# Mixture-of-experts weights: from two-part products on the whole TensorE to float32 products on four 32-column tiles

## The chip, the core and the metric

One core of a Trainium2 chip runs the whole program. The metric is the device time of one execution in microseconds (us). A profile of one execution shows every instruction of the engines: PE is TensorE's matmuls, PEld its weight loads, DVE is VectorE, ACT is ScalarE, POOL is GpSimd, and SP issues the transfers from HBM.

## What is computed

A decoder trunk of two layers over 256 tokens of width 1024. Each layer has a mixer (a gated spatial part and an attention), a channel part, two norms and a gate. The channel part of layer 0 is a dense SwiGLU; that of layer 1 is eight SwiGLU experts, of which every token uses two:

```python
def swiglu(x, w1, w3, w2):
    return (jax.nn.silu(x @ w1) * (x @ w3)) @ w2

def moe(x, w_r, w1, w3, w2):
    ...
    top_l, top_i = lax.top_k(logits, TOP_K)
    top_w = jax.nn.softmax(top_l, axis=-1)
    combine = jnp.sum(jax.nn.one_hot(top_i, N_EXPERTS, dtype=jnp.float32) * top_w[..., None], axis=1)
    ...
    for e in range(N_EXPERTS):
        out = out + combine[:, e:e + 1] * swiglu(xt, w1[e], w3[e], w2[e])
```

An expert's three matrices are 1024 x 3584, 1024 x 3584 and 3584 x 1024, in float32: 44 MB, and 352 MB for all eight. With the inputs of the reference the experts have 74, 61, 64, 40, 50, 69, 94 and 60 tokens.

## The kernel before

The tokens lie in two blocks of 128. A class `Stream` (line 96) holds the order in which all weights are used. A unit of up to 1 MiB is loaded into a buffer of a ring (`load`, line 186), and `take` (line 202) hands out its pieces, 128 rows by 1024 columns each. `_split` (line 127) cuts a piece into two parts of 12 significant bits, high and low: ScalarE copies it to the type fp32r (line 143), VectorE subtracts that copy from the piece (line 145). Both go to one of nine `cut` slots. A raw buffer is free once its last piece is cut, a slot once its piece has been multiplied.

A product of activations and weights is then three fp32r matmuls per 512 columns (`mm3`, line 426: activations' high part by weights' high part, high by low, low by high). In the trace they are the lines L428, L430 and L432; the weights' parts are `hl`.

The experts are computed in `moe` (line 974), one after the other. `gather_block` (line 939) multiplies the tokens by a 0/1 matrix, so that an expert's tokens stand in 128 slots, transposed (`g`, then `xg` in two parts). The hidden width of 3584 is done in 7 chunks of 512. `up` (line 1007) takes 8 pieces, each with 512 columns of w1 and the same of w3, into two PSUM banks (`m`), and makes `mh` = silu times product. `turn` transposes it (`mt`) and `turned` splits it (`mhT`). `down` (line 1030) takes 4 pieces of w2 into two more banks (`py`). `down` of a chunk stands behind `up` of the next, so that `mh` is made while `py` is computed. After an expert's last chunk, `spread` (line 1046) brings its rows back to the tokens (`sc`) and adds them to `acc`. One expert is thus 7 x (8 + 4) = 84 pieces, all eight 672, and a piece costs six matmuls of 512 columns.

PE, DVE and ACT run their instructions in the order of the program, which a scheduler has set; SP issues a unit's transfers when a buffer is free. A branch at the end, `overflow` (line 1102), handles tokens beyond an expert's slots; here no expert has more than 128.

Of the kernel before, what the change touches and what calls it, by code (L numbers as in the profile page):

```python
# [18 lines left out]
P = 128  # L19
# [39 lines left out]
RAW3 = 2  # L59
# [11 lines left out]
LEND = 3  # L71
LEND0 = 4
# [13 lines left out]
SPLITS = 4  # L86
AFT = 1
# [8 lines left out]
class Stream:  # L96
    """Weights in order of use: units of up to 1 MiB are loaded ahead, then cut, piece by piece, into two parts of 12
    significant bits each. Both token blocks take every piece, block 1 some pieces after block 0."""

    def __init__(self, tc, nc, raw, cut):  # L100
        self.tc = tc
        self.nc, self.rings, self.cut = nc, [raw], cut
        self.idle, self.busy, self.lend, self.lent = list(range(SPL)), {}, 0, []
        self.extra = []
        self.room, self.size = [RAW], [RAW]
        self.units, self.pieces, self.lags, self.stays = [], [], [], set()
        self.left = [None]
# [7 lines left out]
        self.highs, self.lows = [], []  # L115

    def add(self, srcs, cuts, gains=None, lag=1):
        """A unit without cuts is only loaded, and stays."""
# [8 lines left out]
    def _split(self, v):  # L127
        u, c0, c1, gain, last = self.pieces[v]
        t, n, nc = self.raws[u], c1 - c0, self.nc
        slot = self.busy[v] = self.idle.pop(0)  # L130
# [19 lines left out]
        if last:  # L150
            r = self.ring.pop(u)
            if isinstance(r, int):
                self.room[r] += 1
            elif r[0] == "cut":
                self.idle.append(r[1])
                self.lent.remove(r[1])
            del self.raws[u]
        self.tiles[v] = (hi, lo)

# [6 lines left out]
    def raw_tile(self, name, stays=False, dtype=F32):  # L166
        """a buffer of a ring that has room, or None."""
# [18 lines left out]
    def load(self, end=None):  # L186
        """Loads the next units, as far as there is room."""
# [10 lines left out]
    def give_back(self):  # L198
        for v in [v for v in self.busy if v < min(self.pos)]:
            self.idle.append(self.busy.pop(v))  # L200

    def take(self, b):
# [3 lines left out]
        while self.n_split < min(j + self.ahead, len(self.pieces) if self.limit is None else self.limit) and self.idle:  # L206
# [10 lines left out]
def side_by_side(st, gens):  # L217
    """Both blocks' programs, block 0 some pieces ahead."""
# [10 lines left out]
def trunk(ctx: ExitStack, tc: tile.TileContext, a, out):  # L229
# [56 lines left out]
    NC = D_FFE // CH  # L286
    steps = [(e, c) for e in range(NE) for c in range(NC)]
    for i in range(DEPTH):
# [15 lines left out]
        else:  # L304
            add_wide(a["ple_w_p"][i], [0], LAG_E)
            st.limit = len(st.pieces) if LIM else None
            def down(e, c):
                add_wide(a["moe_w2"][0, e][c * CH:(c + 1) * CH], range(0, CH // P, 2), 1)
            for s, (e, c) in enumerate(steps):
                add_pair(a["moe_w1"][0, e], a["moe_w3"][0, e], c * CH, CH, 1)  # L310
# [60 lines left out]
    def tables():  # L371
        """gains as columns, the mask, the rotary tables (tokens on partitions)."""
# [27 lines left out]
    def inv_root(name, v, n):  # L400
        """(v + eps) ** -0.5 of [P, n]."""
# [13 lines left out]
    def transposed(name, src, into, k0=0, nk=KT):  # L415
        """token-major [P, nk * P] -> two parts of its transpose."""
# [17 lines left out]
    def product(b, ps, xT, ks, between=iter(()), bias=None):  # L434
        """ps (two banks) = x_b @ w (+ bias, a row); the stream's next pieces are w's rows ks; other work's steps in between."""
# [19 lines left out]
    def half_product(b, ps, xT, between=iter(())):  # L455
        """ps (one bank) = x_b @ w, two rows of tiles in a piece."""
# [11 lines left out]
    def load_rows(key, *srcs):  # L468
        """vectors side by side, on every partition."""
# [34 lines left out]
    def embed_input(i, b, pT):  # L504
        """p[i] of the block, transposed, in two parts."""
# [6 lines left out]
    def embed(i, b, pp):  # L512
        """pp = p[i] @ ple_w_p[i]."""
# [6 lines left out]
    def mixer(i, b, xT):  # L520
        """x_b after the first residual and norm, and its transpose."""
# [53 lines left out]
        if b == 0:  # L575
            # the spatial gate's weights, masked and transposed
# [73 lines left out]
        m = gp.tile([P, 512], F32, name=f"{L}m{b}")  # L650

        def attend():
# [120 lines left out]
    def gated(b, ps, pp, xb):  # L773
        """xb += sigmoid(ps) * pp; the last layer's xb goes out."""
# [8 lines left out]
    def tail(i, b):  # L783
        """second norm and the per-layer embedding's gate."""
# [15 lines left out]
    def program(b):  # L800
        for i in range(DEPTH):
# [4 lines left out]
            else:  # L806
                if YR:
                    yield
                with tc.high_priority(offset=B_ROUTER) if b in BR else nullcontext():
# [4 lines left out]
                    placed = gather_block(tc, b, 0, x, early, rt["pg"], rt)  # L814
                if b == 1:
                    st.limit = None
                    st.after = [] if not LIM else [L_[i]["ends"][1]] * AFT + [placed.ins] * (SPLITS - AFT)
# [16 lines left out]
    moe(tc, a, st, x, acc, xtp, rt, early, ident, const, small, ps_mm, ps_tr, ps_s, mm3, split_from, steps)  # L834
# [8 lines left out]
    def finish(b):  # L843
        """the last norm and gate; acc stays."""
# [17 lines left out]
    def redo(w):  # L862
        """the last norm and gate once more, in whole float32 products."""
# [22 lines left out]
def router_constants(tc, a, rt, const):  # L886
# [6 lines left out]
    # places count from 1  # L893
# [20 lines left out]
def router(tc, b, rt, const, ps_tr):  # L914
    """Every token's two experts and its place among each one's tokens, block after block."""
# [15 lines left out]
    # a token's place among its expert's tokens, from 1 on; 0 where it isn't one  # L931
# [7 lines left out]
def gather_block(tc, b, e, x, pl, pg, rt):  # L939
    """Adds the block's tokens of expert e to the two banks pg, transposed, each in its slot."""  # L940
    nc = tc.nc
    # 1 where a token of the expert stands in a slot
    placed = nc.vector.tensor_scalar(pl[:, b, :], rt["iota"], rt["slot"][:, b, e:e + 1], None, op0=OP.is_equal)
    for k in range(KT):
        # a bank's first product clears it
        nc.tensor.matmul(pg[k // 4][:, k % 4 * P:(k % 4 + 1) * P], lhsT=x[b][:, k * P:(k + 1) * P], rhs=pl[:, b],
# [4 lines left out]
def router_weights(tc, rt, small, const, ps_tr):  # L951
    """The softmax of the two logits, and the largest number of tokens of an expert."""
# [4 lines left out]
    # e = exp(second - first); weights 1 / (1 + e) and e / (1 + e)  # L957
# [16 lines left out]
def moe(tc, a, st, x, acc, xtp, rt, early, ident, const, small, ps_mm, ps_tr, ps_s, mm3, split_from, steps):  # L974
    """acc = alpha * x + experts(x), each expert on its own tokens."""
    nc = tc.nc
    iota, slot = rt["iota"], rt["slot"]
    with tc.tile_pool(name="moe", bufs=1) as mp:

        def gather(e, s):  # L980
            """expert e's tokens, transposed, in the banks of the step s."""
            pl = mp.tile([P, NB, P], F32, tag="place", name=f"place{e}")
            pg = [ps_mm(s % 2, f"g{e}_{q}") for q in range(2)]
# [4 lines left out]
        def gathered(e, pg):  # L988
            """in two parts."""
            xg = [mp.tile([P, KT, P], F32R, tag=f"xg{j}", name=f"xg{j}_{e}") for j in range(2)]  # L990
            for q in range(2):
                split_from(xg[0][:, q * 4:q * 4 + 4].rearrange("p k s -> p (k s)"), xg[1][:, q * 4:q * 4 + 4].rearrange("p k s -> p (k s)"), pg[q])
# [199 lines left out]
```

## Time and profile before

| | |
|---|---|
| median of three timed executions | 1485.36 us (1485.06 to 1485.43) |
| span of the profiled execution, first to last instruction | 1483.9 us |
| PE busy over the span | 1461.2 us, 98% |
| PEld, DVE, ACT busy | 80%, 82%, 66% |
| bytes read from HBM | 428.66 MB, 290 GB/s over the span |

The page's busy time of PE is the union of its matmuls' spans, and these overlap: a matmul is listed with its whole way through the array, while the next one has already begun. How fast PE really works is therefore read from the distance of two starts, not from a duration. The times in a timeline count from the start of the span.

### The profile page before, as it was taken

To read this page: it belongs to the slowest core of one execution; us is meant where nothing else is said; L and a number is where in the kernel's file an instruction comes from. 1 tells how busy PE (TensorE), PEld (TensorE's weight loads), DVE (VectorE), ACT (ScalarE), POOL (GpSimd) and SP (SyncE) were. 2 spreads that over 40 slices of the span, in tenths; PEclk is the share of its full clock that TensorE was granted. 3 is DMA by queue.
4 is the path that set the end of the run, shared out by engine and by line. 5 is a ranking of instruction groups with operands and counts; after the bars stand their busy time and mean duration, and the time that the engine had idled before them with its cause. 6 is when DMAs were issued, how large, how long until landed. Compare 5 with 4: busy or idle time off the path is not lost. (4 is left out here: it accounts for less than half of the span.)

```text
span 1483.9 us, 18910 instructions
## 1 busy us (share of the span) xinstructions
PE 1461.2 (98%) x6858; PEld 1188.8 (80%) x6858; DVE 1214.4 (82%) x1410; ACT 986.6 (66%) x1200; POOL 26.3 (2%) x55
## 2 busy tenths in 40 slices
PE   8999999999999999999999999999999999999997
PEld 7878888788878888888888888788878878887875
DVE  7876545588689989989988888998898899889876
ACT  6754444446468777777777677777677677767662
POOL 1000000000000000000000000000000000000000
PEclk9999999999999999999999999999999999999998
DMA  9535546565599999999999999999999899989820
GB/s 323 192 109 200 175 141 226 188 211 186 202 356 329 361 335 339 373 337 344 357 367 328 330 351 334 326 371 365 331 337 371 320 336 367 370 323 340 317 115 30
DMA packets 187311, 431.00 MB, mean 290 GB/s; under 512 B 12199, under 2 KB 18893, under 8 KB 187214
## 3 DMA queue, kind: packets, MB, share of 16 engines
q1 hardware_dynamic: 187214, 429.76, 80.4%
q8 instruction: 55, 0.90, 0.2%
q14 instruction: 42, 0.34, 0.1%
HBM read 428.66 MB, written 1.05 MB: 290 GB/s over the span
## 5 line engine op out<-in xcount | busy, mean ns | idle before, releaser
L145 DVE TENSOR_TENSOR hl<-raw,hl 128x1024 fp32r<-128x1024 f32 (+2 forms) x783 | 920.8, 1215 | 134.8 <-ACT hl L143 132.2
L143 ACT ACTIVATE hl<-raw 128x1024 fp32r<-128x1024 f32 (+2 forms) x783 | 787.6, 1049 | 214.0 <-PE m L432 62.7
L430 PE MATMUL m<-hl,xg 128*128 128x512 f32 x896 | 285.2, 397 | 1.1 <-DVE hl L145 1.1
L428 PE MATMUL m<-hl,xg 128*128 128x512 f32 x896 | 284.2, 397 | 0.0
L432 PE MATMUL m<-hl,xg 128*128 128x512 f32 x896 | 283.3, 396 | 0.0
L430 PEld LDWEIGHTS m<-hl,xg 128*128 128x128 f32 x896 | 167.6, 188 | 44.8 <-DVE hl L145 5.7
L432 PEld LDWEIGHTS m<-hl,xg 128*128 128x128 f32 x896 | 168.6, 188 | 40.4
L428 PEld LDWEIGHTS m<-hl,xg 128*128 128x128 f32 x896 | 167.3, 188 | 38.9
L428 PE MATMUL py<-hl,mhT 128*128 128x512 f32 x448 | 143.5, 401 | 0.2 <-ACT mhT L409 0.2
L430 PE MATMUL py<-hl,mhT 128*128 128x512 f32 x448 | 143.3, 401 | 0.0
L432 PE MATMUL py<-hl,mhT 128*128 128x512 f32 x448 | 140.9, 395 | 0.0
L432 PEld LDWEIGHTS py<-hl,mhT 128*128 128x128 f32 x448 | 84.2, 188 | 20.1
L430 PEld LDWEIGHTS py<-hl,mhT 128*128 128x128 f32 x448 | 82.1, 188 | 19.0 <-DVE hl L145 1.5
L428 PEld LDWEIGHTS py<-hl,mhT 128*128 128x128 f32 x448 | 81.9, 189 | 18.0 <-ACT mhT L409 0.7
L1015 ACT ACTIVATE mh<-m 128x512 f32<-128x512 f32 x56 | 33.3, 595 | 71.9 <-PE m L432 70.8
L409 ACT ACTIVATE mhT<-mt 128x512 fp32r<-128x512 f32 x56 | 33.4, 597 | 57.2 <-PE py L430 48.4
L1016 DVE TENSOR_TENSOR mh<-mh,m 128x512 f32<-128x512 f32 x56 | 38.4, 686 | 31.7 <-ACT mh L1015 31.5
L428 PE MATMUL ff<-hl,L0x1T 128*128 128x512 f32 (+1 forms) x192 | 57.6, 377 | 0.1
L430 PE MATMUL ff<-hl,L0x1T 128*128 128x512 f32 (+1 forms) x192 | 57.2, 373 | 0.0
L432 PE MATMUL ff<-hl,L0x1T 128*128 128x512 f32 (+1 forms) x192 | 56.3, 373 | 0.0
L409 DVE TENSOR_TENSOR mhT<-mt,mhT 128x512 fp32r<-128x512 f32 x56 | 38.5, 688 | 4.1 <-ACT mhT L409 2.6
L428 PEld LDWEIGHTS ff<-hl,L0x1T 128*128 128x128 f32 x192 | 35.0, 188 | 6.8 <-ACT L0x1T L409 0.5
(478 smaller groups left out, 1435.5 us busy)
## 6 DMA issues: line engine op xcount, KB each, us to landing
raw<-in_moe_w SPq DMA_DIRECT2D x448, 512.0 KB, 5.7
raw<-in_moe_w SPq DMA_DIRECT2D x112, 1024.0 KB, 6.6
raw<-in_ffn_w SPq DMA_DIRECT2D x40, 512.0 KB, 4.5
raw<-in_ffn_w SPq DMA_DIRECT2D x11, 1024.0 KB, 4.8
raw<-in_w_in SPq DMA_DIRECT2D x8, 1024.0 KB, 5.2
raw<-in_w_o SPq DMA_DIRECT2D x8, 1024.0 KB, 5.3
raw<-in_ple_w_g SPq DMA_DIRECT2D x8, 1024.0 KB, 4.9
raw<-in_w_in SPq DMA_DIRECT2D x4, 832.0 KB, 5.4
```

Source lines behind the costliest of these rows:

```text
L143: nc.scalar.activation(hi[:, :n], t[:, c0:c1], AF.Copy)
L145: nc.vector.tensor_tensor(lo[:, :n], t[:, c0:c1], hi[:, :n].bitcast(F32), op=OP.subtract)
L409: return nc.scalar.activation(hi, src, AF.Copy).ins, nc.vector.tensor_tensor(lo, src, hi.bitcast(F32), op=OP.subtract).ins
L428: nc.tensor.matmul(o, lhsT=xh, rhs=w, start=start, stop=False)
L430: nc.tensor.matmul(o, lhsT=xh, rhs=w, start=False, stop=False)
L432: nc.tensor.matmul(o, lhsT=xl, rhs=w, start=False, stop=stop)
L1015: nc.scalar.activation(hh, ps[0], AF.Silu)
L1016: nc.vector.tensor_tensor(hh, hh, ps[1], op=OP.mult)
```

## The change

Only the experts change. The host puts the three matrices of each expert into one array `moe_w`, in units of 1 MiB in the order of use, each unit 128 rows (one for each partition) of 8 KB without gaps (`expert_units`). The stream no longer cuts these pieces: `_split` hands out the raw buffer itself, and it is held until the piece has been multiplied (`whole`, `held`, `let_go`). The `cut` slots, which then stand idle, serve as buffers for loads (LEND and LEND0 are 9).

The products become plain float32 matmuls. An expert has 96 slots in place of 128, and they are three groups of 32. The array's 128 columns are used as four tiles of 32 columns: three of them hold the three groups of tokens, and the fourth holds one of these groups again, for another quarter of the weights. Of a piece's 1024 columns, three quarters of 256 columns (`main`) are multiplied by the three groups each, and the last quarter (`side`) by one group at each of the three turns. So a piece is 3 x 4 = 12 float32 matmuls of 256 columns.

The hidden width is done in chunks of 1024, 1024, 1024 and 512 in place of seven of 512; `up` of 1024 uses four PSUM banks. The rows of an expert go back to the tokens (`spread`) one step later, in float32.

```diff
@@ class Stream
+        if v in self.whole:
+            self.tiles[v] = (t[:, c0:c1], None)
+            if last:
+                self.held[v] = self.ring.pop(u)
+                del self.raws[u]
+            return
...
+        for v in [v for v in self.held if v < min(self.pos)]:
+            self.let_go(self.held.pop(v))
@@ trunk
-RAW3 = 2
+RAW3 = 1
...
-LEND = 3
-LEND0 = 4
+LEND = 9
+LEND0 = 9
...
+            def whole(e, units, cuts):
+                n = len(st.pieces)
+                for u in units:
+                    st.add([(lambda t: t, a["moe_w"][0, e, u])], cuts, None, 1)
+                st.whole.update(range(n, len(st.pieces)))
@@ moe
+        def tiles4(main, side, lhsT, wa, wb, start, stop):
+            for j in range(3):
+                for g in range(NG):
+                    nc.tensor.matmul(main[j][g], lhsT=lhsT(g), rhs=wa[j], start=start and j != 1, stop=stop, skip_group_check=True)
+                nc.tensor.matmul(side[j], lhsT=lhsT(j), rhs=wb, start=start and j != 1, stop=stop, skip_group_check=True)
+        def quads(u, v):
+            at = ((u, 0), (u, H2), (v, 0))
+            main = [[t[g * G:(g + 1) * G, c:c + H2] for g in range(NG)] for t, c in at]
+            return main, [t[NG * G:(NG + 1) * G, c:c + H2] for t, c in at]
         def up(s):
             e, c = steps[s]
...
-                hi, lo = st.take(0)
-                mm3(ps, xg[0][:, k, :], xg[1][:, k, :], [hi[:, :CH], hi[:, CH:]], [lo[:, :CH], lo[:, CH:]], k == 0, k == KT - 1)
...
+                t, _ = st.take(0)
+                for j, (u, v) in enumerate(banks):
+                    main, side = quads(u, v)
+                    c1, c3 = j * CH, w + j * CH
+                    tiles4(main, side, lambda g: xg[:, k, g * G:(g + 1) * G],
+                           [t[:, n:n + H2] for n in (c1, c1 + H2, c3)], t[:, c3 + H2:c3 + CH], k == 0, k == KT - 1)
```

What this does on PE in the middle of `up` shows first. Before, one piece of `up` (the piece `hl_5071`, banks `m_20` and `m_21`) stands in PE's queue as six rows:

```order
L428 MATMUL m_20_5115<-hl_5071,xg_1_4799 128x512
L428 MATMUL m_21_5116<-hl_5071,xg_1_4799 128x512
L430 MATMUL m_20_5115<-hl_5071,xg_1_4799 128x512
L430 MATMUL m_21_5116<-hl_5071,xg_1_4799 128x512
L432 MATMUL m_20_5115<-hl_5071,xg_1_4800 128x512
L432 MATMUL m_21_5116<-hl_5071,xg_1_4800 128x512
```

Now the same amount of weights (1024 of the 2048 columns of the unit `raw_4779`, banks `m_100` and `m_101`) is three turns of one row of three matmuls (L1035, the three groups of tokens by one quarter) and one single one (L1036, the fourth tile). The second and the third turn of the piece, and the first row of the next, are:

```order
L1035 MATMUL m_100_5297<-raw_4779,xg_4884 32x256 x3
L1036 MATMUL m_100_5297<-raw_4779,xg_4884 32x256
L1035 MATMUL m_101_5298<-raw_4779,xg_4884 32x256 x3
L1036 MATMUL m_101_5298<-raw_4779,xg_4884 32x256
L1035 MATMUL m_110_5299<-raw_4779,xg_4884 32x256 x3
```

A row of before fills all 128 columns of the array with one matmul; of now each matmul fills 32 of them, and it reads the raw unit instead of the two cut parts.

The second place is where an expert's rows go back to the tokens. Before, the `sc` products stand between matmuls of the same shape, in the first `up` behind the expert's end:

```order
L428 MATMUL m_11_4971<-hl_4904,xg_1_4799 128x512
L430 MATMUL m_10_4970<-hl_4904,xg_1_4799 128x512
L1070 MATMUL sc_4946<-y_4942,plT_4091 128x512
L430 MATMUL m_11_4971<-hl_4904,xg_1_4799 128x512
L432 MATMUL m_10_4970<-hl_4904,xg_1_4800 128x512
```

Now they stand one step later, and they and the transposes `mt`, which use the array as a whole, stand between matmuls on tiles (`py` ahead, `m` behind):

```order
L1036 MATMUL py_5521<-raw_5080,mhT_5279 32x256
L1072 MATMUL mt_5627<-ident,mh_1_5509 128x96 x4
L1072 MATMUL mt_5633<-ident,mh_1_5509 128x96 x4
L1035 MATMUL m_200_5654<-raw_5106,xg_4884 32x256
L1114 MATMUL sc_5642<-y_5273,plT_4069 128x512
L1114 MATMUL sc_5645<-y_5273,plT_4069 128x512
L1035 MATMUL m_200_5654<-raw_5106,xg_4884 32x256 x2
L1036 MATMUL m_200_5654<-raw_5106,xg_4884 32x256
L1114 MATMUL sc_5648<-y_5273,plT_4069 128x512
```

Going once through an expert, PE leaves the tiles for the whole array eight times: four times for `mt`, twice for `sc`, once for the transposes of the 0/1 matrix (`gt`) and once for the next expert's gather (`g`).

The third place is SP's queue near the beginning of the experts' loads. Before, a unit of w1 and w3 is two transfers of 128 x 2 x 512 elements, and a unit of w2 one of 128 x 2 x 1024:

```order
L194 DMA raw_3522<-in_moe_w 128x2x512 x2
L194 DMA raw_3525<-in_moe_w 128x2x512 x2
L194 DMA raw_3528<-in_moe_w 128x2x1024
L194 DMA raw_3580<-in_moe_w 128x2x512 x2
L194 DMA raw_3702<-in_moe_w 128x2x512 x2
```

Now every unit is one transfer of 128 x 2048, a whole row for each partition:

```order
L210 DMA raw_3516<-in_moe_w 128x2048
L210 DMA raw_3518<-in_moe_w 128x2048
L210 DMA raw_3570<-in_moe_w 128x2048
L210 DMA raw_3691<-in_moe_w 128x2048
L210 DMA raw_3693<-in_moe_w 128x2048
```

The bytes are the same, and the units stand at the same places of the queue.

More of the change, by code (lines that the diff above doesn't have):

```diff
@@ L115, in __init__ @@
         self.highs, self.lows = [], []
+        self.whole, self.held = set(), {}
     def add(self, srcs, cuts, gains=None, lag=1):
@@ L205, in take @@
         self.load()
-        while self.n_split < min(j + self.ahead, len(self.pieces) if self.limit is None else self.limit) and self.idle:
+        while self.n_split < min(j + self.ahead, len(self.pieces) if self.limit is None else self.limit) and (self.idle or self.n_split in self.whole):
             self._split(self.n_split)
@@ L832, in trunk @@
     last = DEPTH - 1
[L834 removed]
+    moe(tc, a, st, x, acc, xtp, rt, early, ident, const, small, ps_mm, ps_tr, ps_s, mm3, split_from)
     st.alone = False
@@ L971, in router_weights, with moe, gather @@
     nc.vector.tensor_copy(rt["most"], mostf)
-def moe(tc, a, st, x, acc, xtp, rt, early, ident, const, small, ps_mm, ps_tr, ps_s, mm3, split_from, steps):
+def moe(tc, a, st, x, acc, xtp, rt, early, ident, const, small, ps_mm, ps_tr, ps_s, mm3, split_from):
     nc = tc.nc
[L977 to L983, printed above, removed]
+    H2 = CH // 2
+    steps = [(e, c) for e in range(NE) for c in range(len(WIDTHS))]
+    last_c = len(WIDTHS) - 1
+    with tc.tile_pool(name="moe", bufs=2) as mp:
+        def gather(e):
+            pl = mp.tile([P, NB, S], F32, tag="place", name=f"place{e}")
+            pg = [ps_tr(f"g{e}_{q}") for q in range(2)]
             for b in range(NB):
@@ new lines, in down, with rows @@
+        def down(s, hT, py):
+            e, c = steps[s]
+            n = WIDTHS[c] // P
+            main, side = quads(*py)
+            for k in range(n):
+                t, _ = st.take(0)
+                tiles4(main, side, lambda g: hT[:, k, g * G:(g + 1) * G], [t[:, j * H2:(j + 1) * H2] for j in range(3)], t[:, 3 * H2:],
+                       c == 0 and k == 0, c == last_c and k == n - 1)
+        def rows(e, py):
+            y = mp.tile([S, D], F32, tag="y", name=f"y{e}", bufs=1)
+            u, v = py
+            nc.scalar.activation(y[:, :CH], u[:S], AF.Copy)
+            nc.vector.tensor_copy(y[:, CH:CH + H2], v[:S, :H2])
+            for g, p in enumerate(quads(u, v)[1]):
+                yg = y[g * G:(g + 1) * G, CH + H2:]
+                if g == 1:
+                    nc.scalar.activation(yg, p, AF.Copy)
+                else:
+                    nc.vector.tensor_copy(yg, p)
+            return y
@@ L1087, in moe, with downs @@
+        pg, pl = rt["pg"], early
+        xg = gathered(0, pg)
+        pys, ys, plTs = {}, {}, {}
+        hT = None
+        def downs(s):
+            e, c = steps[s]
+            if c == 0:
+                pys[e] = [ps_s(f"py{e}{q}") for q in range(2)]
+            down(s, hT, pys[e])
+            if c == last_c:
+                ys[e] = rows(e, pys.pop(e))
         for s, (e, c) in enumerate(steps):
-            if c == NC - 1 and e + 1 < NE:
-                ready[e + 1] = gather(e + 1, s + 1)
```

284 lines of the change are left out of this document (142 added, 142 removed).

## The prediction

> **What bounds the kernel now.** I read the windows first, to see which part of the time the change can touch. The row of a stretch gives PE, PEld, DVE and ACT busy, PE's granted clock, the share of the 16 transfer engines and their rate:
>
> ```profile
> core 0: us, PE busy (x) PEld busy (x) DVE busy (x) ACT busy (x) POOL busy (x), PEclk, DMA share, GB/s
> 430.40:1440.40 1010.00, 1008.66 (x4557) 815.49 (x4556) 893.20 (x858) 742.00 (x820) 0.00 (x0) 1.00 0.93 339
> 1440.40:1483.90 43.50, 34.24 (x129) 22.99 (x128) 28.19 (x40) 14.32 (x19) 1.82 (x2) 0.90 0.07 25
> ...
> 1200.00:1300.00 100.00, 99.74 (x454) 80.22 (x454) 89.92 (x87) 73.32 (x82) 0.00 (x0) 1.00 0.98 356
> ```
>
> The experts take 1010 of 1483.9 us, at full clock. PE is never idle there, DVE is busy 88%, and the transfers run at 0.93, up to 0.98. Three resources stand near their limit, so I ask which one is waited for. The groups by line of that stretch tell it, behind the last bar: the idle time of the engine, and what ended it.
>
> ```profile
> L145 DVE TENSOR_TENSOR hl<-raw,hl 128x1024 fp32r<-128x1024 f32 x668 | 786.4, 1222 | 56.5 <-ACT hl L143 54.0
> L143 ACT ACTIVATE hl<-raw 128x1024 fp32r<-128x1024 f32 x667 | 670.1, 1054 | 99.7 <-PE m L432 62.7 <-DVE hl L145 26.2 <-PE py L432 9.3
> L430 PE MATMUL m<-hl,xg 128*128 128x512 f32 x896 | 285.2, 397 | 1.1 <-DVE hl L145 1.1
> L428 PE MATMUL m<-hl,xg 128*128 128x512 f32 x896 | 284.2, 397 | 0.0
> L432 PE MATMUL m<-hl,xg 128*128 128x512 f32 x896 | 283.3, 396 | 0.0
> L430 PE MATMUL py<-hl,mhT 128*128 128x512 f32 x448 | 143.3, 401 | 0.0
> ```
>
> PE waits 1.1 us in all for DVE; ACT waits for PE, since a slot comes free when PE is done with it. **PE bounds this stage**, and neither the cutting nor the loads do. What freeing DVE and ACT gives is therefore next to nothing by itself, and the time of the change is decided on PE. A duration of 397 ns says little about that; the timeline gives the pace:
>
> ```profile
> 702.00 0.63 PE L428 MATMUL m<-hl,xg 128*128 128x512 f32 x2
> ...
> 702.47 0.63 PE L430 MATMUL m<-hl,xg 128*128 128x512 f32 x2
> ...
> 702.94 0.63 PE L432 MATMUL m<-hl,xg 128*128 128x512 f32 x2
> ```
>
> Two matmuls start every 0.47 us, so one takes 0.2345 us. There are 3 x 896 + 3 x 448 = 4032 of them: 945.5 us of the 1010.
>
> **The products of the weights.** Whole float32 matmuls exist in the trace of before, so their price can be read. The gather (L946, 128 columns) and the last expert's `sc` (L1070, 512 columns) are such; each product is recorded as two matmuls. The rows of PEld mark starts too, since a load is listed as the matmul before it begins:
>
> ```profile
> 528.70 3.73 PE L946 MATMUL g<-place,x 128*128 128x128 f32 x32
> ...
> 1444.38 1.98 PE L1070 MATMUL sc<-y,plT 128*128 128x512 f32 x4
> ...
> 1444.92 0.19 PEld L1070 LDWEIGHTS sc<-y,plT 128*128 128x128 f32 x1 [0.24 <-DVE acc L1071]
> 1445.34 0.19 PEld L1070 LDWEIGHTS sc<-y,plT 128*128 128x128 f32 x1 [0.24 <-issue]
> ...
> L946 PE MATMUL g<-place,x 128*128 128x128 f32 x224 | 26.1, 275 | 0.0
> ...
> L1070 PE MATMUL sc<-y,plT 128*128 128x512 f32 x64 | 24.1, 427 | 0.0
> ```
>
> A record of 128 columns costs (3.73 - 0.28) / 31 = 0.111 us, one of 512 columns 0.42 to 0.43. Between them lie 0.83 ns for a column, so a record of 256 columns is 0.217 us, and a product, two records, 0.434. The bounds: 0.213 if only its columns count (half of 0.426), and 0.234 if it pays what L428 pays, 0.2345 for 512 columns at half that price for a column, 21 ns more than its columns. I take 0.217, the nearest rows being float32 themselves.
>
> A turn has four products on four tiles. If the tiles really work at the same time, a turn costs one product, 0.434, and a piece three turns, 1.302 us; the six matmuls of before cost 1.407. That is the whole gain: the columns are the same (3 x 256 x 4 passes against 6 x 512), and only the 21 ns for each matmul go. With 672 pieces: 945.5 - 672 x 1.302 = **-70.6 us**. No row of before shows two tiles at once; that the four share the array is the assumption on which all hangs, and its opposites are rivals below.
>
> Could issuing be slower than that? A turn has 8 records with 8 loads, 54 ns for a pair.
>
> ```profile
> 445.01 0.20 PE L967 MATMUL counts<-sel,ones 128*128 128x8 bf16 x2
> ```
>
> Here two pairs start some 30 ns apart (0.20 less the 0.17 that one lasts), so the queue can deliver. A load of 32 columns isn't in the trace; between nothing and the 0.111 of 128 columns (the gather's pace, which its loads may set) I take a quarter, hidden behind 0.217.
>
> **What else stands on PE.** `sc` was 7 x 8 fp32r matmuls, 56 x 0.2345 = 13.1 us, and becomes 7 x 4 float32 products of two records, 28 x 0.86 = 24.1: **+11 us**; the last expert's stay. Gather and transposes keep their number and their price (the load of 128 columns decides): 0.
>
> Eight times in an expert PE leaves the tiles and comes back, 64 round trips. Now, with one width, such a place is free:
>
> ```profile
> 526.41 0.63 PE L432 MATMUL py<-hl,mhT 128*128 128x512 f32 x2
> 526.88 0.60 PE L1022 MATMUL mt<-ident,mh 128*128 128x128 f32 x4
> 527.23 0.71 PE L428 MATMUL py<-hl,mhT 128*128 128x512 f32 x2
> 527.78 0.63 PE L430 MATMUL py<-hl,mhT 128*128 128x512 f32 x2
> ...
> L1015 ACT ACTIVATE mh<-m 128x512 f32<-128x512 f32 x56 | 33.3, 595 | 71.9 <-PE m L432 70.8
> L1016 DVE TENSOR_TENSOR mh<-mh,m 128x512 f32<-128x512 f32 x56 | 38.4, 686 | 31.7 <-ACT mh L1015 31.5
> ```
>
> From 526.88 to 527.78 four transposes and two matmuls start, 0.90 us; less 0.47 for the matmuls, a transpose takes 0.11 and nothing is lost. If the array must run empty between a tile's matmul and one of full width, it is different: a matmul of 128 columns lasts 0.275 (L946 above) while its successor starts after 0.111, so 0.164 us of overlap goes at each switch, 0.33 for a round trip, **+21 us**. The bounds are 0, as now, and 0.71, if the load of the next weights (0.19 in PEld's rows) is held back as well on both ways: 0 to 45 us. The rule that speaks for a price is in the Trainium skill, page "TensorEngine Tiling (Array Packing)", section "Key Properties": "Changing tiling mode (not just tile) drains the TensorE"; no run here shows it. By that rule the sum has such a term, without it the sum would be 21 us lower.
>
> `gt` and the first `sc` stand one tile's matmul behind `mt` and need its PSUM bank, which ACT and DVE must first copy out (0.6 us, L1015). Some 0.3 us of that show each time, 16 times: **+5 us**. The bounds are 0 and 1 us each.
>
> **What is hidden.** 667 cuts on ACT and DVE go; they were waited for 1.1 us. New on DVE are multiplications of 32 x 256 to make `mh`; at under 0.4 us each (0.69 for 512 columns, L1016), six to a step, they lie beside a `down` of 5 to 10 us, and if that cover went, PE would wait some 3 us in each of 32 steps. At the first step there is no `down`: +1 us. The overflow branch is not entered: 94 tokens is the most, and there are 96 slots. What starts behind the experts (43.5 us in the window above) stays.
>
> **The loads** have the same bytes:
>
> ```profile
> raw<-in_moe_w SPq DMA_DIRECT2D x448, 512.0 KB, 5.7
> raw<-in_moe_w SPq DMA_DIRECT2D x112, 1024.0 KB, 6.6
> ...
> 386.01 12.60 SPq L194 DMA_DIRECT2D raw<-in_moe_w  x11
> ```
>
> 448 x 0.524 + 112 x 1.049 = 352.3 MB. The window at 1200 has 356 GB/s at a share of 0.98, so full engines bring 363 GB/s: 970 us from the first load at 386, to 1356. PE would be done with the experts at 1440.4 - 33 = 1407, 50 us later. Rows of 8 KB instead of 2 and 4 may go faster or as now; either way they lie under PE, with up to 20 buffers ahead (4 + 5 + 1 of the rings, 9 slots and one more). Were PE faster by more than these 50 us, the loads would be late next.
>
> **The sum:** -70.6 + 11 + 21 + 5 + 1 = -33 us. The profiled execution spans 1483.9, so 1451; the median of the runs is 1.5 us above that span: **1452 us**.
>
> **Rivals.** First, the tiles share the array, but every record costs the 21 ns over its columns that L428 pays on top, 0.238: 4032 records one behind the other (3 turns x 2 x 672) by 0.021 us are +85, **1537**. For it speaks that each matmul of the weights pays that now, against it that the float32 rows don't. It decides from 33 / 4032 = 8 ns for a record on, where the gain is gone: the kernel is then **slower** than before.
>
> Second, the two records of one product use the same 32 columns and stand next to each other. If a record that must wait for its columns holds all behind it, only the second record of a product and the first of the next overlap. A turn then costs four times 0.217, 0.868: 2016 turns by 0.434 more are +875, **2327**. For it speaks that in every quoted row PE's matmuls start in the order of the queue; against it nothing in before, where no record could have overtaken another. The Trainium skill, page "TensorE: Matmul & The Clock Gate", section "The mechanism", states that rule: matmuls begin and end strictly in program order, also on different tiles. By it the time would be this rival's; the traces so far agree without having tested it.
>
> Third, the tiles don't share the array at all, and the change doesn't do what it says: a turn is 8 x 0.217, 2016 x 1.302 more, **4077**.
>
> Fourth, the switches and the banks cost nothing and a record just its columns: 1452 - 26 - 4032 x 0.004 = **1410**, and there the loads (1356 and 3 us for the last unit's pieces, then 43.5 and 1.5: 1404) are as late as PE.
>
> **How the numbers follow.** The forecast has 62%, with its own range of 1415 to 1500 (switches from 0 to 45, waits from 0 to 16, a record from 0.213 to 0.225 us, not all at one end together). A measurement of this kernel can tell about 0.2%, 3 us, from no change: of the 62, 53 are faster, 3 the same and 6 slower. The first rival has 12%, the second 16, the third 3, the fourth 7. Faster: 53 + 7 = 60; same: 3; slower: 6 + 12 + 16 + 3 = 37. The range from 1400 to 1545 holds the forecast, the first and the fourth, 81%.
>
> **What would show it.** In the changed profile, in the middle of `up`, the starts of one column tile's records should follow each other every 0.217 us while three others run: 8 records in 0.434 us. 0.868 would be the second rival, 1.74 the third, 0.476 the first. The distance from the last `py` matmul to the first `m`, less four or eight transposes, gives the price of a switch. DVE and ACT should fall under a fifth of the stage, and transfers should wait for buffers, not PE for transfers: a PE that waits for `raw` would make the forecast wrong on the side of the loads.

## The result and the profile after

| | before | after |
|---|---|---|
| median | 1485.23 us | 1443.25 us (1442.83 to 1443.68) |
| ratio to before | | 0.9716, 95% interval 0.9702 to 0.9729 |
| span of the profiled execution | 1483.9 us | 1441.6 us |
| experts, first `m` to last `py` | 430.5 to 1440.0: 1009.6 us | 429.8 to 1397.0: 967.2 us |
| PEld, DVE, ACT busy over the span | 80%, 82%, 66% | 66%, 32%, 21% |

The change is 42.0 us faster, 2.8%; the forecast was 33 us. All of it lies in the experts: they begin 0.7 us earlier, last 42.4 us less, and what stands behind them lasts some 0.8 us more. The windows of the changed kernel (PE, PEld, DVE and ACT busy, granted clock, share and rate of the transfers) answer to those of before:

```profile
429.70:1397.20 967.50, 967.41 (x16653) 577.51 (x16652) 144.91 (x317) 68.64 (x125) 0.00 (x0) 1.00 0.91 353
...
1200.00:1300.00 100.00, 100.00 (x1706) 60.15 (x1698) 16.51 (x36) 6.24 (x12) 0.00 (x0) 1.00 0.94 364
```

PE is as full as before. DVE fell from 88% of the stage to 15%, ACT from 73% to 7%, and no engine used what they left. The groups of the same stretch say behind the last bar who waits:

```profile
L1035 PE MATMUL m<-raw,xg 128*32 128x256 f32 x8064 | 599.3, 380 | 0.1
L1036 PE MATMUL m<-raw,xg 128*32 128x256 f32 x2688 | 589.6, 380 | 0.0
...
L1062 DVE TENSOR_TENSOR mh<-mh,m 32x256 f32<-32x256 f32 x168 | 71.2, 424 | 3.3
L1058 ACT ACTIVATE mh<-m 96x512 f32<-96x512 f32 x56 | 33.2, 593 | 579.2 <-PE m L1036 561.6 <-issue 17.6
...
L1114 PE MATMUL sc<-y,plT 96*128 96x512 f32 x56 | 27.8, 618 | 0.0
```

PE's products waited 0.1 us; ACT waits for PE, and DVE has more than 800 us of the stage to spare. The queue of the transfers waits for PE too. Its waits, as total, number and longest, have at their head:

```profile
SPq L210 <- PE m L1036: 553.7, 219, 9.9
SPq L210 <- PE py L1036: 257.2, 103, 9.1
```

So PE bounds the stage still, and the time was decided on its pace. That is in the timeline in the middle of an `up` (start, duration, count):

```profile
700.09 0.38 PE L1036 MATMUL m<-raw,xg 128*32 128x256 f32 x1
700.10 0.58 PE L1035 MATMUL m<-raw,xg 128*32 128x256 f32 x3
700.31 0.38 PE L1036 MATMUL m<-raw,xg 128*32 128x256 f32 x1
700.32 0.58 PE L1035 MATMUL m<-raw,xg 128*32 128x256 f32 x3
```

A record is one row of a matmul in the trace; a float32 product is two. The fourth tile (L1036) starts a record every 0.2155 us (0.431 for two), and three others (L1035) go beside it. Call such a set of four records a step. In the program's order a turn is six records of L1035 and then two of L1036; here every step has three of the one and one of the other, so records start ahead of older ones whose tile is busy, and the sentence ahead of the prediction that PE runs its instructions in the order of the program does not hold for matmuls on different tiles. A turn of 8 records costs 0.431 us, as forecast (0.434). The durations say nothing of that: 16128 records of 380 ns make 6100 us, six times the stage.

### The profile page after: what moved, and what is told of

It reads as the page before. It is cut to its first block, busy times and chain, and to the rows that moved or that the text cites. A ratio compares the mean times of both kernels' runs of the same rounds, so it can differ in the third digit from the quotient of the medians.

```text
span 1441.6 us, 40785 instructions
## 1 busy us (share of the span) xinstructions
PE 1418.4 (98%) x18954; PEld 950.5 (66%) x18954; DVE 463.9 (32%) x876; ACT 305.7 (21%) x496; POOL 25.8 (2%) x55
## 3 DMA queue, kind: packets, MB, share of 16 engines
HBM read 428.66 MB, written 1.05 MB: 298 GB/s over the span
## 5 line engine op out<-in xcount | busy, mean ns | idle before, releaser
L1035 PE MATMUL m<-raw,xg 128*32 128x256 f32 x8064 | 599.3, 380 | 0.1
L1036 PE MATMUL m<-raw,xg 128*32 128x256 f32 x2688 | 589.6, 380 | 0.0
L1035 PEld LDWEIGHTS m<-raw,xg 128*32 128x32 f32 x8064 | 334.4, 110 | 241.6 <-issue 14.3
L1035 PE MATMUL py<-raw,mhT 128*32 128x256 f32 x4032 | 299.2, 379 | 0.0
L1036 PE MATMUL py<-raw,mhT 128*32 128x256 f32 x1344 | 295.5, 379 | 0.0
L1036 PEld LDWEIGHTS m<-raw,xg 128*32 128x32 f32 x2688 | 293.2, 110 | 0.0
L1035 PEld LDWEIGHTS py<-raw,mhT 128*32 128x32 f32 x4032 | 169.1, 110 | 115.4 <-ACT mhT L1077 0.8
L1058 ACT ACTIVATE mh<-m 96x512 f32<-96x512 f32 x56 | 33.2, 593 | 579.2 <-PE m L1036 561.6
L159 DVE TENSOR_TENSOR hl<-raw,hl 128x1024 fp32r<-128x1024 f32 (+2 forms) x111 | 129.7, 1173 | 78.1 <-ACT hl L157 78.1
L1036 PEld LDWEIGHTS py<-raw,mhT 128*32 128x32 f32 x1344 | 147.3, 110 | 0.0
L157 ACT ACTIVATE hl<-raw 128x1024 fp32r<-128x1024 f32 (+2 forms) x111 | 112.8, 1021 | 113.2 <-PE ff L458 54.9
L1062 DVE TENSOR_TENSOR mh<-mh,m 32x256 f32<-32x256 f32 x168 | 71.2, 424 | 3.3
L454 PEld LDWEIGHTS ff<-hl,L0x1T 128*128 128x128 f32 x192 | 35.1, 188 | 6.8 <-ACT L0x1T L435 0.5
L456 PEld LDWEIGHTS ff<-hl,L0x1T 128*128 128x128 f32 x192 | 35.1, 188 | 6.2
L458 PEld LDWEIGHTS ff<-hl,L0x1T 128*128 128x128 f32 x192 | 34.9, 188 | 6.5 <-DVE L0x1T L435 0.2
L1114 PE MATMUL sc<-y,plT 96*128 96x512 f32 x64 | 31.7, 618 | 0.0
```

Source lines behind the costliest of these rows:

```text
L157: nc.scalar.activation(hi[:, :n], t[:, c0:c1], AF.Copy)
L159: nc.vector.tensor_tensor(lo[:, :n], t[:, c0:c1], hi[:, :n].bitcast(F32), op=OP.subtract)
L454: nc.tensor.matmul(o, lhsT=xh, rhs=w, start=start, stop=False)
L456: nc.tensor.matmul(o, lhsT=xh, rhs=w, start=False, stop=False)
L458: nc.tensor.matmul(o, lhsT=xl, rhs=w, start=False, stop=stop)
L1035: nc.tensor.matmul(main[j][g], lhsT=lhsT(g), rhs=wa[j], start=start and j != 1, stop=stop, skip_group_check=True)
```

## The experiments

All kernels are the changed one with one edit, where nothing else is said; the kernel before ran beside them on the same chip. `e2`, `e1b`, `e11`, `e5` and `e10` were timed once each; what is read from them is far larger than the spread of the others, except between `e5` and `e10`.

**What the tiles give, and in which order they take records**

`e2_full_width` has the products without tiles, 96 columns and 512 columns of weights at once (the code that reads `m` and `py` follows that form, and its part of the diff is left out here):

```diff
-            for j in range(3):
-                for g in range(NG):
-                    nc.tensor.matmul(main[j][g], lhsT=lhsT(g), rhs=wa[j], ...)
-                nc.tensor.matmul(side[j], lhsT=lhsT(j), rhs=wb, ...)
+            for ps, w in zip(main, wa):
+                nc.tensor.matmul(ps, lhsT=lhsT, rhs=w, start=start, stop=stop)
```

> The changed kernel without tiles: each float32 product takes 96 columns and 512 columns of weights at once, two products for a piece in place of twelve. Theory: four tiles work at the same time and this is the whole gain of the products; a piece is then 2 products x 2 records x 0.43 us = 1.72 us instead of 1.293 us, 672 pieces cost 287 us more, and some 24 us of switches between tiles and the whole array go: about 1706 us. Rival: the shared tiles bring little, and float32 products are cheap in themselves; then it stays under 1500 us.

Measured: 1703.5 us. The theory holds: float32 alone would have made this kernel slower by 218 us, and the tiles give back 260. A piece at 1.293 us is three quarters of 1.72: 96 slots leave 32 of the 128 columns idle, and the fourth tile is what uses them.

`e1_by_tile` does the same products with a tile's three in a row:

```diff
-            for j in range(3):
-                for g in range(NG):
+            for g in range(NG):
+                for j in range(3):
                     nc.tensor.matmul(main[j][g], ...)
-                nc.tensor.matmul(side[j], ...)
+            for j in range(3):
+                nc.tensor.matmul(side[j], ...)
```

> The products of the changed kernel in another order: within a piece all three products of the first tile (six records), then of the second, the third, the fourth. The work is the same. Theory: the tiles share the array because a record overtakes older ones whose tile is busy; if that reaches over a whole piece (24 records), the time is that of the changed kernel, 1443 us within 4. First rival: records start in program order; then only the last record of one tile and the first of the next overlap, a piece is 20 steps of 0.2155 us instead of 6, and 672 pieces cost 2028 us more: 3470 us. Second rival: overtaking reaches only a few records; the time lies between, and its place tells how many. If six in a row on one tile are too many, three tiles stand still in part of each piece.

Measured: 1847.5 us, ratio 1.2435 (1.241 to 1.246). Neither the theory nor the first rival, but the second. Its timeline (the fourth tile is L1037 here):

```profile
700.13 0.38 PE L1035 MATMUL m<-raw,xg 128*32 128x256 f32 x1
700.16 0.38 PE L1037 MATMUL m<-raw,xg 128*32 128x256 f32 x1
700.17 0.56 PE L1035 MATMUL m<-raw,xg 128*32 128x256 f32 x2
700.38 0.38 PE L1037 MATMUL m<-raw,xg 128*32 128x256 f32 x1
700.41 0.38 PE L1035 MATMUL m<-raw,xg 128*32 128x256 f32 x1
700.60 0.38 PE L1037 MATMUL m<-raw,xg 128*32 128x256 f32 x1
```

From 700.13 to 700.60 six records start, three in each step of 0.22 to 0.23 us: three tiles work, one is idle. That makes 1.85 us for a piece instead of 1.293, some 370 us of the 404; the tiles also end unevenly, and the way from the last turn to a transpose is 0.77 us here instead of 0.33.

`e9_pairs_by_tile` has runs of four records, `e1b_by_tile_unit` runs of twelve where an `up` has two bank pairs (48 of 84 pieces):

```diff
+            for js in ((0, 1), (2,)):
+                for g in range(NG):
+                    for j in js:
+                        nc.tensor.matmul(main[j][g], ...)
+                for j in js:
+                    nc.tensor.matmul(side[j], ...)
```

> As the order by tile of before, but with runs of four records on one tile (two products) for two thirds of the work, and of two for the rest. With runs of six, three records were at work at any time. A model: records of the oldest unfinished one and of the 9 to 12 behind it may start as soon as their tile is free. It gives three at a time for runs of six, and four at a time for runs of four: the time of the changed kernel, 1443 us within 5. Rival: any run longer than one product costs, in proportion: then a good part of the 404 us that runs of six cost comes back, some 150 to 270 us, 1590 to 1710 us.

> The order by tile with runs of twelve records on one tile in the 48 of an expert's 84 pieces that have a second bank pair (the up of 1024 columns), and runs of six in the other 36. The model of a reach of 10 to 13 records, counted from the oldest that is unfinished, gives two tiles at work at any time for runs of twelve: 12 steps of 0.2155 to 0.231 us for a piece, 2.59 to 2.77 us, where runs of six take 1.89. Then 8 x 48 x (0.69 to 0.88) more than the 1847 us of runs of six alone: 2113 to 2183 us. Rival: a reach that is counted in products or by the tiles' own queues, six records each or more; then three tiles stay at work and the time stays near 1847 us. Rival on the other side: no more than the next run is seen once runs are long, 2.3 records a step less than two: over 2300 us.

Measured: 1448.65 us with runs of four (ratio 0.975, 0.9731 to 0.977), 0.4% over the changed kernel: four tiles are at work, but they end unevenly, and the way to a transpose grew from 0.33 to 0.40 us. With runs of twelve 2482 us: the model of a reach over 10 to 13 records fell, and the last rival came nearest. The timeline (the fourth tile is L1044):

```profile
825.18 0.40 PE L1044 MATMUL m<-raw,xg 128*32 128x256 f32 x1
825.39 0.38 PE L1042 MATMUL m<-raw,xg 128*32 128x256 f32 x1
825.42 0.38 PE L1044 MATMUL m<-raw,xg 128*32 128x256 f32 x1
...
825.82 0.38 PE L1042 MATMUL m<-raw,xg 128*32 128x256 f32 x1
825.85 1.46 PE L1044 MATMUL m<-raw,xg 128*32 128x256 f32 x6
826.93 0.40 PE L1042 MATMUL m<-raw,xg 128*32 128x256 f32 x1
```

The fourth tile begins its twelve at 825.18, while the tile ahead still has three more to start. Then it works alone, and the next tile begins only at 826.93, when four of the fourth tile's twelve are left: the one that starts with it and three more. So the records that wait seem to be held per tile, one at work and three waiting, and a full tile stops the hand-out for all. By this, a run of n is followed by the next after n - 4 steps: four tiles for runs of four, 3.0 for six, 1.5 for twelve, as seen. `e11_four_then_two` tests it with runs of eight and four in those 48 pieces:

> A new model from the three orders so far (four tiles at work with runs of four records on a tile, three with runs of six, 1.47 with runs of twelve): records are handed out in program order, a tile holds one at work and three waiting, and the hand-out stops at a record whose tile is full, though other tiles are idle. Tested with runs that it has not seen: in the 48 pieces of an expert with the second bank pair, two pieces as a run of eight records on each tile and then a run of four on each; the other 36 pieces as in the changed kernel. The model gives 4 x 4 steps for the eights and 4 for the fours, 20 steps of 0.2155 to 0.225 us for two pieces, 2.16 to 2.25 us for one in place of 1.293: 384 pieces cost 333 to 367 us more, 1776 to 1811 us, and up to 15 more for tiles that end unevenly at the switches. Rival: one store of five waiting records for all four tiles, which gives three tiles with runs of six and 1.7 with runs of twelve: 18 steps, 1690 to 1730 us. Rival: a reach of 10 to 13 records from the oldest unfinished: 16 to 18 steps, 1600 to 1730 us.

Measured: 1812.1 us, within the model's range (1776 to 1811, and up to 15 more for the switches) and outside both rivals'. In its trace a unit of two pieces lasts 4.44 us, 20 steps of 0.222.

**What the layout gives**

`e3_layout_alone` is the kernel before with the host's units of 1 MiB; `e4_products_alone` loads the changed kernel's units from the three arrays.

```diff
 # before.py, e3_layout_alone
-                add_wide(a["moe_w2"][0, e][c * CH:(c + 1) * CH], range(0, CH // P, 2), 1)
+                packed(e, range(6 * c + 4, 6 * c + 6))
...
-                add_pair(a["moe_w1"][0, e], a["moe_w3"][0, e], c * CH, CH, 1)
+                packed(e, range(6 * c, 6 * c + 4))
 # after.py, e4_products_alone
-                    st.add([(lambda t: t, a["moe_w"][0, e, u])], cuts, None, 1)
+                    st.add(pieces_of(e, u), cuts, None, 1)
```

> The kernel before with the experts' weights laid out by the host in units of 1 MiB, rows of 8 KB, in the order of use; cuts, slots and products as before. Theory: PE bounds the kernel before and waits 1.1 us in all for the cuts, so faster loads change nothing: 1485 us within 3. Rival: part of the gain is the layout, through fewer packets beside PE's reads; then up to 20 us less, about 1465.

> The changed kernel with the weights loaded from the three arrays of before: rows of 4 KB for most units of w1, w3 and w2, of 2 KB for an expert's last chunk. Products as in the changed kernel. An expert lasts 121.5 us there, so 44 MB need 362 GB/s. Theory: full engines brought 363 GB/s with the rows of before, with 20 units of buffers ahead, so PE still waits for nothing or for next to nothing: 1443 to 1448 us. Rival: the layout carries the gain; the loads then stay behind PE by more, expert after expert (with 340 GB/s, 129.6 us for an expert, 8 x 8 us less the buffers' 50: 1460 us or more).

Measured: 1484.8 us (ratio 0.9995, 0.9985 to 1.0004) and 1441.9 us (0.9702, 0.9686 to 0.9718, against 0.9702 to 0.9729 with the layout). The second is 1 us under the range that was expected. The layout brings nothing that can be measured, with either kind of products. Its effect is seen in the windows all the same: the first row is of the layout alone, where the share was 0.93 before; the second of the products alone, where it is 0.91 with the layout.

```profile
430.40:1440.40 1010.00, 1008.65 (x4558) 814.57 (x4557) 893.13 (x858) 742.11 (x820) 0.00 (x0) 1.00 0.88 339
```

```profile
429.70:1397.20 967.50, 967.36 (x16655) 577.47 (x16655) 145.06 (x318) 69.27 (x126) 0.00 (x0) 1.00 0.94 354
```

The same bytes take less of the transfer engines with rows of 8 KB; nothing waits for it.

**Where the loads become the bound**

`e5_two_turns` leaves out the second of three turns, `e10_two_turns_rows` does so with the rows of the three arrays:

```diff
-            for j in range(3):
+            for j in (range(3) if start else (0, 2)):
```

> The changed kernel with the second of the three turns of a piece left out, except in the first row block of each accumulation; its output is not the reference's. PE's products fall by nearly a third, some 275 of 869 us; the loads stay. It shows where the loads become the bound. Theory: the loads are the next wall: 352.3 MB from 386 us on. By the rate of the changed kernel (364 GB/s at a share of 0.94, 387 at full share) they end at 1296, and with 3 us for the last unit, 44 us behind the experts and 1.5 us outside of the span the time is about 1345 us; by the rate that the prediction took (363 GB/s) 1404 us. Rival: nothing but PE bounds; then about 1170 us.

> The kernel with two turns of three (its output is not the reference's) with the weights loaded from the three arrays of before, rows of 4 KB, and of 2 KB for an expert's last chunk. With rows of 8 KB that kernel was bound by its loads, 415 to 419 GB/s, 1291 us. Theory: the rows set the rate of full engines; with the rate seen with these rows beside whole products (355 GB/s at a share of 0.94, 378 at full share) 352.3 MB take 932 us from 386 us on, and with 48 us behind it 1367 us (1345 to 1400). Rival: the rate doesn't depend on the rows but on how many transfers are under way; then 1291 us within 10.

Measured: 1291.0 and 1316.5 us. The loads bound both, as expected, but well below the times of both theories, and the second is outside its rival too. The windows of the two, 8 KB rows first, and the head of the first one's waits of PE:

```profile
600.00:1100.00 500.00, 442.12 (x7040) 239.47 (x7036) 87.28 (x189) 37.04 (x70) 0.00 (x0) 1.00 1.01 418
```

```profile
600.00:1100.00 500.00, 466.16 (x6850) 266.65 (x6846) 86.18 (x189) 37.30 (x71) 0.00 (x0) 0.98 1.02 402
```

```profile
PE m L1035 <- DMA raw<-in_moe_w: 48.8, 90, 1.9
```

Now PE waits for `raw`, and the engines bring 418 GB/s, with rows of 4 and 2 KB 402. In the second PE waits less for `raw`, 20.7 us, but its loads run without a break too (a share of 1.02), and the queue waits for earlier loads to land (524.7 us). The 4% between the two rates come from one run each, the second at a granted clock of 0.98. A share of 0.98 at 356 GB/s, which the prediction took for full engines, was no ceiling. That could have been read in the trace of before, where the first loads of the experts, with rows of 2 and 4 KB, went faster:

```profile
400.00:420.00 20.00, 19.37 (x100) 15.80 (x99) 14.28 (x32) 7.55 (x11) 1.83 (x2) 1.00 1.04 391
```

So the share of these windows can pass 1, and 0.98 of it is not the same as full.

**What the switches cost**

`e6_side_work_on_tiles` puts the gather, `gt` and `sc` on column tiles; `e7_one_place` leaves them whole and emits `gt` and `sc` together inside an expert's second `up`; `e8_rows_on_tiles` has both edits for `gt` and `sc`, and the gather whole.

```diff
 # e6, e8 (e6 has the same for g)
-                    nc.tensor.matmul(ps, lhsT=plT[:, b], rhs=y[:, cs], start=True, stop=True)
+                    for i in range(0, P, G):
+                        nc.tensor.matmul(ps[i:i + G], lhsT=plT[:, b, i:i + G], rhs=y[:, cs], ...)
 # e7, e8
             for k in range(KT):
+                if k == 4 and inside:
+                    inside()
```

> The changed kernel with the gather, the products that bring rows back and the turning of the 0/1 matrix on column tiles of 32 as well (that turning by float32 products with the identity, two records); the transposes of the hidden rows stay on the whole array. Of 8 round trips between tiles and the whole array in an expert 4 stay. Theory: it is the change of the tile size that costs at each such place (in the trace 0.115 us on the way out and 0.09 on the way back beside what one starts there anyway, and 0.12 for a turn that is broken apart): per expert 0.2 for the gather, 0.4 for the 0/1 matrix, 2 x 0.42 for the rows, 1.45 in all, so some 11 us less, and up to 7 us more from the gather's pace: 1425 to 1434 us. Rival: the gaps come from waiting for data or banks at these places, not from the size; then 1443 us within 3.

> The changed kernel with the turning of the 0/1 matrix and the rows' way back in one place, in the middle of the second up of an expert and between whole turns, still on the whole array. Three round trips and three broken turns in an expert become one round trip. Theory: this saves two round trips and the broken turns, about 1.23 - 0.2 = 1.0 us an expert, 7 to 8 us: 1435 to 1437 us. Rival: the products then wait for PSUM banks that VectorE must first read (0.75 us each), and the time stays at 1443 us within 3 or rises.

Measured: 1438.7 us (ratio 0.968, 0.9664 to 0.9696) and 1438.3 us (0.9678, 0.9662 to 0.9694). Both gain 5 us, less than expected, and for different reasons. In the first, PE has new waits in the stage (total, number, longest):

```profile
PE g L972 <- issue: 3.8, 4, 1.3
PE py L1038 <- issue: 2.3, 2, 1.6
PE py L1037 <- issue: 1.7, 2, 1.3
```

7.8 us in which PE waited for nothing that the profile shows, in the gather or some 5 us behind it. The changed kernel has none; the gather's 32 records, 0.11 us apart, have become 128, which come every 20 ns. The trace's packets point to a cause: its queue `instruction` brings 16 KB at a time, some 7 us apart, and each of the eight stops ends 1.3 to 1.6 us after such a packet has landed. So PE seems to have waited for its instructions; no edit tested that. With 7.8 us less the time would be 1431 us, inside the expected range. In the second the place is not one yet:

```profile
702.44 0.42 PE L1024 MATMUL gt<-ident,place 128*96 128x128 f32 x2
702.70 1.88 PE L1116 MATMUL sc<-y,plT 96*128 96x512 f32 x4
704.51 0.62 PE L1035 MATMUL m<-raw,xg 128*32 128x256 f32 x2
705.06 1.98 PE L1116 MATMUL sc<-y,plT 96*128 96x512 f32 x4
```

One product of `up` still stands between the halves of `sc`, alone on the array, with a switch on either side. So an expert saves one round trip and one broken turn instead of two and three; by the prices worked out below, 0.29 and 0.43 us, that is 5.0 us in seven experts, and 4.9 were measured.

> As the kernel with one place, and in that place the turning of the 0/1 matrix and the rows' way back are on column tiles of 32; the gather stays on the whole array, where its few long loads start no burst of instructions. Theory: switches cost what the trace showed, and the 7.7 us of waits for instructions that the gather on tiles brought are not met here. In the kernel with one place this stretch lasts 4.85 us (0.23 of it a product of up); now 16 records groups of 0.43 in fours, that is 4 x 0.86, and 0.45 for the 0/1 matrix and the last turn, 3.9 us: 0.7 us less in each of 7 experts and as much at the end, 5 us less than 1438.3: 1432 to 1435 us. Rival: what the switches took is taken by the waits for the PSUM banks, since four products on two banks now stand side by side: 1438 us within 2, or more.

Measured: 1433.7 us (0.9652, 0.9639 to 0.9665): 9.5 us better than the changed kernel, its interval clear of that kernel's, and the fastest of the kernels that leave nothing out. The place in its timeline, without a switch and without waits:

```profile
701.36 0.50 PE L1025 MATMUL gt<-ident,place 128*32 128x128 f32 x9
701.59 0.62 PE L1118 MATMUL sc<-y,plT 96*32 96x512 f32 x1
701.68 0.28 PE L1025 MATMUL gt<-ident,place 128*32 128x128 f32 x3
701.79 3.84 PE L1118 MATMUL sc<-y,plT 96*32 96x512 f32 x31
705.45 0.40 PE L1036 MATMUL m<-raw,xg 128*32 128x256 f32 x3
```

From the first `gt` to the next `m` it is 4.1 us; in the kernel with one place it was 4.5, with one product of `up` in it, and there a switch on either side besides.

## Why the prediction was right, and where its sizes were off

The forecast was 1452 us in a range of 1400 to 1545, and the time is 1443. Its steps:

- **PE bounds, cuts and loads do not**: right on both sides. The layout alone gave nothing. That freeing DVE and ACT gives nothing by itself was not run alone; it rests on the 1.1 us for which PE waited on them before.
- **Products, -70.6 us**: 4032 steps of 0.2155 us are 868.9, and 945.5 less that makes -76.6 us. The record of 256 columns had been put between two float32 rows at 0.217; it pays 2 ns over the 0.213 of its columns. The 21 ns of the first rival are not there.
- **`sc`, +11 us**: 56 records at 0.43 us in place of 56 at 0.2345, as worked out.
- **Switches, +21 us**: there, at 0.29 us for a round trip where 0.33 was forecast. The last step of a `down`, the next `mt`, and the way back:

```profile
517.73 0.39 PE L1035 MATMUL py<-raw,mhT 128*32 128x256 f32 x3
517.75 0.38 PE L1036 MATMUL py<-raw,mhT 128*32 128x256 f32 x1
518.06 0.88 PE L1072 MATMUL mt<-ident,mh 96*128 96x96 f32 x8
518.87 0.42 PE L1035 MATMUL m<-raw,xg 128*32 128x256 f32 x3
...
519.11 0.39 PE L1035 MATMUL m<-raw,xg 128*32 128x256 f32 x3
```

What the same transposes and `sc` cost without a change of the tile size stands in the trace of `e2_full_width`, where all products use the whole array:

```profile
609.23 1.02 PE L1034 MATMUL py<-raw,mhT 128*96 128x512 f32 x2
610.09 0.83 PE L1065 MATMUL mt<-ident,mh 96*128 96x96 f32 x8
610.75 1.02 PE L1034 MATMUL m<-raw,xg 128*96 128x512 f32 x2
...
653.69 1.88 PE L1099 MATMUL sc<-y,plT 96*128 96x512 f32 x4
655.41 1.02 PE L1034 MATMUL m<-raw,xg 128*96 128x512 f32 x2
```

There eight transposes take 0.66 us from the first start to the next `m`, and nothing is lost ahead of them. In the changed kernel the way from the last step to `mt` is 0.33 us where the next step would have come after 0.2155, the transposes take 0.81 us, and the first step behind them 0.24: 0.115 + 0.15 + 0.025 = 0.29 us. Four records of `sc` take 1.72 us there and 1.91 here; with both ends a round trip is 0.32. For all 63 it comes to some 18 us. By the rule from the Trainium skill, page "TensorEngine Tiling (Array Packing)", section "Key Properties", a change of the tiling mode drains the array; the trace agrees, and without such a price the sum would be lower by these 18 us. Something like it stood in the trace of before, where the prediction saw none. There two records with one row stand between `sc` records of 128 rows:

```profile
1443.33 1.12 PE L438 MATMUL fin<-raw,one 1*128 1x512 f32 x2
```

From their first start to that of the next `sc`, at 1444.38, it is 1.05 us, where two records of `sc` take 0.86. Whether this change of rows is the same thing was not tried.

- **What the sum lacked**: a turn broken apart by a switch. One product, two records, goes alone:

```profile
603.86 0.62 PE L1035 MATMUL m<-raw,xg 128*32 128x256 f32 x2
604.41 1.98 PE L1114 MATMUL sc<-y,plT 96*128 96x512 f32 x4
606.32 0.41 PE L1035 MATMUL m<-raw,xg 128*32 128x256 f32 x2
```

Its two records follow each other on one tile while three tiles stand idle, and the six that are left of the turn take two steps again. That is two steps more, 0.43 us, for each of 15 broken turns, 6.5 us: the trace has 4062 steps in place of 4032.

- **Transposes, 0**: they did not keep their price. Four took 0.43 us before, with what was lost behind them; with 96 tokens and float32 on both sides eight take 0.66 us (`e2` above). For 224 of them that is 5.5 us less.
- **Waits for banks, +5 us, and the first step, +1 us**: none; the waits of PE have no row in the stage. The first `sc` starts 0.31 us behind the last record of `up`, just as `mt` does behind `py`, so only the switch stands between them. Where a wait was expected, single products of `up` stand, and they are the broken turns.

The sum by measured terms is -76.6 + 11 + 18 + 6.5 - 5.5; with 2 us for the slow start below and 1 us for a product that stood behind the experts before (L464), it is about -44 us, and the stage lost 42.4. The 1 or 2 us between were not taken apart. That the forecast came within 9 us is partly luck: it had the products, switches, transposes, banks and first step too dear by some 21 us, and lacked some 9 us for the broken turns, the slow start and L464.

96 slots in place of 128 and chunks of 1024 in place of 512 were not tried alone; by this sum little is left for them besides the transposes.

- **The second rival** (a record that waits holds all behind it, 2327 us) had 16%. It did not come for this order, though it was right in kind: the hand-out does stop, but only at a fifth record on one tile, and the changed kernel puts two there before it goes on. The Trainium skill, page "TensorE: Matmul & The Clock Gate", section "The mechanism", has matmuls begin strictly in program order, on different tiles too. Here the measurement differs: by that rule a turn would be 0.868 us, and it is 0.431.
- **The loads** as the next wall at 1404 us: the mechanism was right, the size off, since 0.98 at 356 GB/s was taken for full engines. The wall is at 1291 us with this layout and about 1316 with rows of 4 and 2 KB, as the kernels with two turns show. For the forecast it made no difference, since the loads stayed under PE either way.

## What to carry to other kernels

Where the rows of activations leave a part of the array's columns idle (here 32 of 128), column tiles can give that part other weights: a piece then cost 1.293 us in whole float32 products instead of 1.72, and less than the 1.407 of two-part weights. Each tile should get no more than four records (two float32 products) before the next tile's turn. Work of another tile size between them costs 0.3 us for each way out and back, and 0.43 more where it breaks a turn apart; keep such work together, or on tiles of the same size. Before a layout is changed for the sake of the loads, look whether anything waits for them: a transfer share of 0.98 was no sign of it.

## What was not expected of the hardware

- Each column tile holds four records, one at work and three waiting, and the fifth stops the hand-out for all tiles: inferred from four orders, and tested on one new one (1812 us, forecast 1776 to 1826).
- With the gather on column tiles, PE met stops of up to 1.6 us (7.8 us in all), for which the waits of the profile name no cause. That instructions arrived too late in that burst fits the landing of the instruction packets, 1.3 to 1.6 us before each stop ends; it was not tried.
- The price of a switch between the whole array and column tiles of 32, 0.26 to 0.33 us for a round trip, shows only beside a kernel with the same work and one tile size; the waits of the profile list none of it.
- PE starts the experts at half pace. The granted clock from 426 to 433 us, first in the changed kernel, then in the kernel before:

```profile
426.00:433.00 7.00, 6.73 (x48) 4.91 (x52) 1.91 (x9) 1.77 (x2) 0.00 (x0) 0.53 1.01 419
```

```profile
426.00:433.00 7.00, 6.10 (x28) 5.49 (x28) 5.23 (x9) 2.02 (x3) 0.00 (x0) 0.76 0.61 219
```

Both kernels come from a wait of 1.5 us on PE and begin the gather at half pace. Before, the second product of the weights ran at its full pace; now the first eight steps on tiles take 0.427 us instead of 0.2155, some 1.8 us in all. Why the clock came back later was not tried.
